# A convolution layer whose shared tap sum moves to ScalarE and GpSimd, one chunk ahead, with the running sum in PSUM

## The chip, the cores and the metric

The kernel runs on one core of a Trainium2 chip. A core has five engines with a queue each: TensorE (PE, matmuls), VectorE (DVE), ScalarE (ACT), GpSimd (POOL) and SyncE (SP), which issues the DMA transfers here. The engines work side by side and wait for one another by semaphores; within its queue each works in order. Two on-chip memories matter: SBUF, and PSUM with its eight banks of 128 x 512 float32, into which TensorE writes its products. The metric is the device time in microseconds from one launch; lower is better.

## The reference

A trunk of two layers over 1024 tokens of 1024 features. Layer 0 mixes tokens with a Conformer convolution, layer 1 with forgetting attention; each is followed by a cross-attention into 256 memory tokens and a squared-ReLU MLP. Only the convolution is touched:

```python
def conformer_conv(h, w_pw1, b_pw1, w_dw, b_dw, ln_g, ln_b, w_pw2, b_pw2):
    u = h @ w_pw1 + b_pw1
    a, gate = jnp.split(u, 2, axis=-1)
    u = a * jax.nn.sigmoid(gate)
    u = lax.conv_general_dilated(
        u, w_dw[:, None, :].astype(u.dtype),
        window_strides=(1,), padding=[(CONV_WIDTH - 1, 0)],
        dimension_numbers=("NWC", "WIO", "NWC"),
        feature_group_count=D_MODEL) + b_dw
    u = jax.nn.silu(layernorm(u, ln_g, ln_b))
    return u @ w_pw2 + b_pw2
```

## The kernel before

Features lie on the 128 partitions, so the 1024 features are eight chunks (`NCH`); tokens lie along the free axis, in two halves of 512. `X` holds the residual stream, one tile of 128 x 512 for each chunk and half. Float32 operands of the large products are split into a high and a low part (`split`, `low`, L147 to L152), and a product is three passes of matmuls, 128x128 by 128x512, summed in a PSUM bank (`product`, L266).

`conv_layer` (L293) normalizes `X` into `hs`, and then goes through the chunks:

- *The gate* (`gated_unit`, L362): for each half two products of 24 matmuls each, the gate first. ScalarE takes the sigmoid from the bank into `sg`, VectorE multiplies it with the other product (L370) into `u`, which keeps even and odd tokens in two planes with 15 zeros of padding in front of each (L301). There are two tiles `u`. The weights of the next chunk are loaded and split one chunk ahead (`gate_weights`).
- *The taps* (`convolve`, L386). Even and odd outputs share work: `d0` and `d1` are differences of neighbouring tokens (L393, L394), `both` is the sum over the odd plane with the pairwise tap sums (`tap_sums`), one product with the bias and 15 multiply-adds (L396, L400), and each of the two outputs then adds its own filters over the differences to it, 16 and 15 multiply-adds (L408). All of it is on VectorE; the running sums of the two outputs lie in two tiles of `X`, and the two runs of instructions alternate.
- Each finished chunk is added to `acc` (L354) for the layer norm's mean.

After the chunks `layer_norm` (L306) runs over both halves, and `linear` multiplies with `pw2` (L360).

Between the chunks the kernel prepares matrices for the two cross-attentions (`memory_matrices`, L433), which need nothing from the convolution: a generator, `prep`, with 32 steps, four for each of four heads and two layers: keys `kt`, values `vt`, then four results `o` from `wq` (L483) and four from `wo` (L501), each stored to DRAM by SP. Its products are in float32 with two matmul records each. Two steps are drawn in each pass over the chunks, four before them, the rest after the layer norm. They have four PSUM banks (`prep_pools(4)`), the gate has two (`banks(2)`), and two more serve small sums and broadcasts.

The order of each engine's instructions is fixed when the program is built. A list scheduler does it: what is traced earlier goes first among what is ready by the scheduler's own clock, and later work fills gaps. On the chip each queue keeps that order.

Of the kernel before, what the change touches and what calls it, by code (L numbers as in the profile page):

```python
# [12 lines left out]
F32 = mybir.dt.float32  # L13
F32R = mybir.dt.float32r
AF = mybir.ActivationFunctionType
ALU = mybir.AluOpType
# [3 lines left out]
P = 128  # L20
D = 1024
S = 1024
NCH = D // P
HALF = 512
# [6 lines left out]
TAPS = 31  # L31
PAD = TAPS - 1
# [4 lines left out]
HALVES = (slice(0, HALF), slice(HALF, S))  # L37
# [49 lines left out]
def trunk(ctx, tc, a, out):  # L87
    nc = tc.nc
    act, dve, pool, pe = nc.scalar, nc.vector, nc.gpsimd, nc.tensor
# [14 lines left out]
    def col(name, i):  # L104
        return par[:, COLS[name] + i : COLS[name] + i + 1]
# [22 lines left out]
    def open_x():  # L128
        xp = xpool.enter_context(tc.tile_pool(name="x", bufs=1, side="right", reuse_waits="tile"))
        return Halves(xp)  # L130

    def load_x(x, src, sl):
        for c in range(NCH):
            nc.sync.dma_start(x[:, c, sl], src[:, c, sl])

    X = open_x()
# [4 lines left out]
    def bank(p):  # L141
        return p.tile([P, HALF], F32, name="mm", tag="mm")

    def banks(n):
        return tc.tile_pool(name="pm", bufs=n, space=PSUM, reuse_waits="tile")
# [8 lines left out]
    def token_mean(acc):  # L154

        m = bank(ps)[:, : acc.shape[-1] // P]
        for b in range(m.shape[-1]):
            pe.matmul(m[:, b : b + 1], acc[:, b * P : (b + 1) * P], mean_col, start=True, stop=True)
        return m

    def spread(v):

        nb = v.shape[-1]
        r = bank(ps)
        with tc.high_priority(offset=SMALL_FIRST):
            for b in range(nb):
                pe.matmul(
                    r[:, b * P : (b + 1) * P], v[:, b : b + 1].to_broadcast([P, P]), ident,
                    start=True, stop=True,
                )  # L170
        return r[:, : nb * P]
# [56 lines left out]
    def operand_tile(p):  # L228
        return p.tile([P, 2, 2, HALF], F32R, name="op", tag="op")

    def operands():

        return [
            [t[:, i].rearrange("p h n -> p (h n)") for i in range(2)]
            for t in (operand_tile(opool) for _ in range(NCH))
        ]
# [53 lines left out]
        dve.tensor_tensor(X[:, m, sl], t, X[:, m, sl], op=ALU.add)  # L290


    def conv_layer(pm, prep):  # L293
        with tc.tile_pool(name="conv", bufs=2) as cp:
            for sl in HALVES:
                next(prep)
                load_x(X, a["xT"], sl)
            def padded():

                u = cp.tile([P, 2, (PAD + S) // 2], F32, name="u")  # L300
                pool.memset(u[:, :, : PAD // 2], 0.0)  # L301
                return u

            pairs = tap_sums(cp)

            def layer_norm(s, acc):  # L306

                nm = nrm.tile([P, 4], F32, name="nm")
                with tc.high_priority(offset=SMALL_FIRST):
                    dve.tensor_scalar(nm, token_mean(acc), -1.0, None, op0=ALU.mult)  # L310
                nmb = spread(nm)
                C = [X[:, m, HALVES[s]] for m in range(NCH)]
                for c in C:
                    dve.tensor_tensor(c, c, nmb, op=ALU.add)
                rb = spread(inverse_rms(C, LN_EPS))
                for m, c in enumerate(C):
                    dve.tensor_tensor(c, c, rb, op=ALU.mult)
                    act.activation(c, c, AF.Silu, bias=col("ln_b", m), scale=col("ln_g", m))
                    split(*(y.rearrange("p (n s) -> p s n", s=2)[:, s, :] for y in ss[m]), c)

            def add_x(m, sl, t):
                x = nrm.tile([P, HALF], F32, name="x", tag="t", bufs=4)
                nc.sync.dma_start(x, a["xT"][:, m, sl])
                dve.scalar_tensor_tensor(
                    X[:, m, sl], t, col("pw2_b", m), x, op0=ALU.add, op1=ALU.add
                )

            def gate_weights(m):
                return [weights(a["pw1"][2 * m + j]) for j in (1, 0)]

            hs = operands()
            ahead = gate_weights(0)
            u = padded()
            for sl in HALVES:
                normalize(hs, "mix0", sl)
                next(prep)
                gated_unit(pm, cp, 0, ahead, hs, u[:, :, PAD // 2 :], sl)
            acc = [cp.tile([P, HALF], F32, name=f"acc{s}", bufs=1) for s in range(2)]
            for m in range(NCH):
                if m:  # L340
                    u = padded()
                    for sl in HALVES:
                        gated_unit(pm, cp, m, ahead, hs, u[:, :, PAD // 2 :], sl)
                if m + 1 < NCH:
                    ahead = gate_weights(m + 1)
                for _ in range(2):
                    next(prep, None)

                convolve(cp, m, u, pairs[:, m])
                for s, sl in enumerate(HALVES):  # L350
                    if m == 0:
                        act.copy(acc[s], X[:, m, sl])
                    else:
                        dve.tensor_tensor(acc[s], acc[s], X[:, m, sl], op=ALU.add)  # L354
            ss = operands()
            for s in range(2):
                layer_norm(s, acc[s])
            for _ in prep:
                pass
            linear(pm, lambda m: weights(a["pw2"][m]), NCH, ss, add_x)  # L360

    def gated_unit(pm, cp, m, ws, hs, u, sl):  # L362
        sg = cp.tile([P, HALF], F32, name="sg")
        for j, w in zip((1, 0), ws):
            t = bank(pm)
            product(t, by_weights(w, hs, sl))
            if j:
                act.activation(sg, t, AF.Sigmoid, bias=col("pw1_b", NCH + m))
            else:
                dve.scalar_tensor_tensor(  # L370
                    u[:, :, sl.start // 2 : sl.stop // 2],
                    t.rearrange("p (n s) -> p s n", s=2), col("pw1_b", m),
                    sg.rearrange("p (n s) -> p s n", s=2), op0=ALU.add, op1=ALU.mult,
                )

    def tap_sums(cp):

        n = TAPS // 2
        w = par[:, COLS["dw_w"] : COLS["dw_w"] + NCH * TAPS].rearrange("p (m t) -> p m t", m=NCH)
        sums = cp.tile([P, NCH, n + 1], F32, name="sums", bufs=1)  # L380
        dve.tensor_copy(sums[:, :, n : n + 1], w[:, :, 2 * n :])
        two = w[:, :, : 2 * n].rearrange("p m (t s) -> p m t s", s=2)
        dve.tensor_tensor(sums[:, :, :n], two[:, :, :, 0], two[:, :, :, 1], op=ALU.add)
        return sums

    def convolve(cp, m, u, sums):  # L386


        n, k = S // 2, TAPS // 2
        even, odd = u[:, 0, :], u[:, 1, :]  # L390
        d0 = cp.tile([P, n + k], F32, name="d0")
        d1 = cp.tile([P, n + k - 1], F32, name="d1")
        dve.tensor_tensor(d0, even[:, : n + k], odd[:, : n + k], op=ALU.subtract)  # L393
        dve.tensor_tensor(d1, even[:, 1 : n + k], odd[:, : n + k - 1], op=ALU.subtract)  # L394
        both = cp.tile([P, n], F32, name="both")
        dve.tensor_scalar(  # L396
            both, odd[:, :n], sums[:, 0:1], col("dw_b", m), op0=ALU.mult, op1=ALU.add
        )
        for j in range(1, k + 1):
            dve.scalar_tensor_tensor(  # L400
                both, odd[:, j : j + n], sums[:, j : j + 1], both, op0=ALU.mult, op1=ALU.add
            )
        out = [X[:, m, sl] for sl in HALVES]
        for s, d, taps in ((0, d0, k + 1), (1, d1, k)):
            y = both
            for j in range(taps):
                w = col("dw_w", m * TAPS + 2 * j + s)
                dve.scalar_tensor_tensor(  # L408
                    out[s], d[:, j : j + n], w, y, op0=ALU.mult, op1=ALU.add
                )  # L410
                y = out[s]

# [13 lines left out]
    @contextmanager  # L428
    def prep_pools(n):
        with tc.tile_pool(name="prep", bufs=2) as pp, tc.tile_pool(name="pps", bufs=n, space=PSUM) as pq:  # L430
            yield pp, pq
# [928 lines left out]
            od[head // 2, i * HD : (i + 1) * HD, (b - 1) * P : (b + 1) * P], ol  # L1360
        )

    with prep_pools(4) as pools, banks(2) as pm:
        conv_layer(pm, chain(*(memory_matrices(*pools, l) for l in range(2))))
    sums = mem_attention(0)
    xd = dram.tile([P, NCH, S], F32, name="xd")
    first_normalized, first_weights = [], []
# [3 lines left out]
    for sl in HALVES:  # L1371
        rb = firsts if sl.start == 0 else spread(rms_of_sums(seconds, RMS_EPS))
        for c in range(NCH):
            y = X[:, c, sl]
# [71 lines left out]
```

## Time and profile before

| what | value |
|---|---|
| median of 3 runs | 2823.84 us (2814.29 to 2826.63) |
| profiled execution | 2825.31 us |
| its span, first to last instruction | 2823.3 us |
| mean granted TensorE clock | 0.991 |
| convolution layer: gates, taps and preparation | 60 to 395 us |
| layer norm | 389 to 443 us |
| product with `pw2` | to about 530 us |

A row of a group reads: line, engine, operation, output <- inputs, shape and count, then busy time, the mean of one in ns, and the idle time before it with what ended it. A row of the timeline reads: start, duration, engine, line, operation, count. The profile calls the weight load of a matmul PEld; it runs beside the matmuls.

### The profile page before, as it was taken

The page shows a single profiled execution, that of the slowest core. Times are in us where ns is not written, and L with a number is a line of the kernel's source. Part 1 is how long each engine was busy: PE and PEld are TensorE (multiplying, and loading weights), DVE is VectorE, ACT ScalarE, POOL GpSimd, SP SyncE. Part 2 cuts the span into 40 slices and gives each one's busy share as a digit, 9 for nine tenths or more (in the row PEclk, how much of TensorE's full clock was granted, in tenths as well). Part 3 has the DMA queues.
Part 4 walks back from the last instruction along what each step waited for, and adds up shares of the span by engine and source line. Part 5 has one row for each costly group of instructions (what it writes and reads, how often), then busy time and mean ns, then how long its engine had stood idle before and what let it go on. Part 6 is the DMA issues. An engine that isn't in the chain of part 4 may idle for free.

```text
span 2823.3 us, 36214 instructions
## 1 busy us (share of the span) xinstructions
PE 2740.8 (97%) x12968; PEld 2261.3 (80%) x12968; DVE 2030.9 (72%) x3358; ACT 1278.3 (45%) x2293; POOL 703.1 (25%) x473
## 2 busy tenths in 40 slices
PE   8999999999999999999899999989999999989998
PEld 6777777888888877888688888878888788878886
DVE  5999984555776576777788888875546855577776
ACT  5212143433555553333466666673423655543332
POOL 0000000000065625774000000000000365525773
PEclk9999999999999999999899999999999999999999
DMA  6334364322165585652222221243213455655651
GB/s 219 120 119 135 114 206 124 101 90 70 65 230 177 178 309 187 227 199 89 69 68 70 57 65 55 69 136 98 94 64 105 149 176 190 218 208 197 227 201 61
DMA packets 165428, 390.68 MB, mean 138 GB/s; under 512 B 17264, under 2 KB 46192, under 8 KB 164992
## 3 DMA queue, kind: packets, MB, share of 16 engines
q1 hardware_dynamic: 165248, 388.37, 40.9%
q8 instruction: 102, 1.67, 0.2%
q14 instruction: 78, 0.64, 0.1%
HBM read 270.79 MB, written 113.31 MB: 136 GB/s over the span
## 4 chain that ended last, share of the span: by engine, by line
PE 74%; DVE 12%; ACT 5%; DMA 5%; issue 3%; POOL 1%; SPq 0%; DVEq 0%; POOLq 0%; ACTq 0%
PE mm L1070 34%; PE mm L269 29%; PE mm L1255 5%; DVE w L148 2%; DVE op L148 2%; DVE x L408 1%; PE mm L1341 1%; DVE x L1310 1%; DMA ua<-x 1%; ACT x L1315 1%; PE mm L1353 1%; PE mm L1354 1%; DVE both L400 1%; DVE wl L148 1%; ACT pth L151 1%
## 5 line engine op out<-in xcount | busy, mean ns | idle before, releaser
L1070 PE MATMUL mm<-op,w 128*128 128x512 f32 x5424 | 1242.4, 391 | 24.5 <-ACT m L955 8.7
L1070 PEld LDWEIGHTS mm<-op,w 128*128 128x128 f32 x5424 | 1020.5, 189 | 243.2 <-ACT m L955 9.6
L269 PE MATMUL mm<-op,wh 128*128 128x512 f32 x1056 | 330.5, 394 | 4.2 <-DVE op L148 4.2
L148 DVE TENSOR_TENSOR w<-r,w 128x512 fp32r<-128x512 f32 x264 | 262.6, 998 | 30.5 <-ACT w L653 30.5
L653 ACT CAST w<-r 128x512 fp32r<-128x512 f32 x264 | 163.3, 622 | 262.0 <-PE mm L1070 233.2
L269 PEld LDWEIGHTS mm<-op,wh 128*128 128x128 f32 x1056 | 200.2, 190 | 48.5 <-DVE op L148 6.5
L1255 PE MATMUL mm<-op,wh 128*128 128x512 f32 x736 | 231.4, 396 | 0.0
L148 DVE TENSOR_TENSOR w<-t,w 128x512 fp32r<-128x512 f32 x180 | 178.2, 1005 | 63.2 <-ACT w L653 63.1
L269 PE MATMUL mm<-op,wl 128*128 128x512 f32 x528 | 210.5, 400 | 7.1 <-DVE wl L148 6.2
L207 POOL TENSOR_TENSOR r<-v,mhalf 128x4 f32<-128x4 f32 (+1 forms) x15 | 16.8, 1117 | 741.0 <-DVE v L205 741.0
L647 POOL TENSOR_TENSOR t<-r,t 128x512 f32<-128x512 f32 x104 | 174.9, 1681 | 91.4 <-DVE w L148 54.2
L653 ACT CAST w<-t 128x512 fp32r<-128x512 f32 x180 | 112.0, 622 | 169.8 <-PE mm L1070 140.6
L151 ACT CAST wh<-raw 128x1024 fp32r<-128x1024 f32 x96 | 100.7, 1050 | 193.8 <-PE mm L269 97.5
L865 POOL TENSOR_TENSOR x<-x,x 128x512 f32<-128x512 f32 x112 | 160.2, 1455 | 112.6 <-ACT x L878 101.6
L967 DVE TENSOR_TENSOR x<-mm,x 128x512 f32<-128x512 f32 x160 | 109.5, 684 | 91.1 <-PE mm L1070 73.7
L1255 PEld LDWEIGHTS mm<-op,wh 128*128 128x128 f32 x736 | 139.2, 189 | 26.7
L269 PE MATMUL mm<-op,xsh 128*128 128x512 f32 x512 | 158.0, 393 | 0.0
L1255 PE MATMUL mm<-op,wl 128*128 128x512 f32 x368 | 155.0, 421 | 1.9 <-ACT q L1275 1.9
L151 ACT CAST pth<-mm 128x512 fp32r<-128x512 f32 (+1 forms) x224 | 105.9, 495 | 108.5 <-PE mm L556 80.8
L408 DVE SCALAR_TENSOR_TENSOR x<-d,par,x 128x512 f32<-128x512 f32 x232 | 154.5, 746 | 0.0
L647 POOL TENSOR_TENSOR t<-r,r 128x512 f32<-128x512 f32 x52 | 80.2, 1542 | 295.1 <-DMA r<-in_ff_w 191.0
L1315 ACT ACTIVATE x<-x,nb 128x128 f32<-128x128 f32 (+7 forms) x128 | 99.5, 778 | 109.3 <-DVE nb L1313 100.0
(188 smaller groups left out, 4689.6 us busy)
## 6 DMA issues: line engine op xcount, KB each, us to landing
r<-in_ff_w SPq DMA_DIRECT2D x128, 512.0 KB, 4.0
op<-ua SPq DMA_DIRECT2D x80, 512.0 KB, 6.8
us<-x SPq DMA_DIRECT2D x128, 256.0 KB, 2.9
op<-us SPq DMA_DIRECT2D x64, 512.0 KB, 5.6
raw<-mvo SPq DMA_DIRECT2D x32, 512.0 KB, 3.4
ua<-ul SPq DMA_DIRECT2D x64, 256.0 KB, 2.2
ua<-uh SPq DMA_DIRECT2D x60, 256.0 KB, 2.3
raw<-in_pw SPq DMA_DIRECT2D x24, 512.0 KB, 4.7
```

Source lines behind the costliest of these rows:

```text
L148: dve.tensor_tensor(lo, src, hi.bitcast(F32), op=ALU.subtract)
L151: act.copy(hi, src)
L269: pe.matmul(out_ps, x, y, start=i == 0, stop=i == len(terms) - 1)
L400: dve.scalar_tensor_tensor(both, odd[:, j : j + n], sums[:, j : j + 1], both, op0=ALU.mult, op1=ALU.add)
L408: dve.scalar_tensor_tensor(out[s], d[:, j : j + n], w, y, op0=ALU.mult, op1=ALU.add)
L647: (dve if g in (2, 3, UP, UP + 1) else pool).tensor_tensor(t, raws[g, x], raws[g, y], op=ALU.subtract)
L653: act.copy(highs[n][0], raws[steps[n][:2]])
L865: eng.tensor_tensor(u[g, x], y1, y2, op=op_)
L967: dve.tensor_tensor(v, sums[key], v, op=ALU.add)
L1070: pe.matmul(sums[key], y, z, start=first and i == 0, stop=n == last_of[key] and i == len(terms) - 1, skip_group_check=True,)
L1255: pe.matmul(t, x, y, start=n == 0, stop=n == len(terms) - 1)
L1315: act.activation(x[:, :n], x[:, :n], AF.Exp, bias=nb, accum_out=rs)
```

## The change

The shared sum `both` leaves VectorE: `shared_sum` computes its 16 terms, ScalarE each product (`Identity` with scale and bias for the first, `Copy` with scale for the others, into six tiles `tap`), GpSimd the 15 additions. It is traced one chunk ahead of `convolve`. The gate is traced two chunks ahead, so there are three planes, padded once before the loop. In `convolve` the running sum of each output lies in one PSUM bank, `acc` of the pool `pc`, and only the last tap writes `X`; both outputs use the same bank in turn. `d0` and `d1` have one buffer each for two. The preparation's PSUM banks are three for four. The loop has one more pass, at m = -1, which gates chunk 1 and draws two preparation steps more.

```diff
-    def conv_layer(pm, prep):
+    def conv_layer(pm, pc, prep):
...
-            def padded():
-
-                u = cp.tile([P, 2, (PAD + S) // 2], F32, name="u")
+
+            planes = [cp.tile([P, 2, (PAD + S) // 2], F32, name=f"u{i}", bufs=1) for i in range(3)]
+            for u in planes:
                 pool.memset(u[:, :, : PAD // 2], 0.0)
-                return u
...
+            def gate(m, ws, sl):
+                gated_unit(pm, cp, m, ws, hs, planes[m % 3][:, :, PAD // 2 :], sl)
+
             hs = operands()
             ahead = gate_weights(0)
-            u = padded()
             for sl in HALVES:
                 normalize(hs, "mix0", sl)
                 next(prep)
-                gated_unit(pm, cp, 0, ahead, hs, u[:, :, PAD // 2 :], sl)
+                gate(0, ahead, sl)
             acc = [cp.tile([P, HALF], F32, name=f"acc{s}", bufs=1) for s in range(2)]
-            for m in range(NCH):
-                if m:
-                    u = padded()
-                    for sl in HALVES:
-                        gated_unit(pm, cp, m, ahead, hs, u[:, :, PAD // 2 :], sl)
-                if m + 1 < NCH:
-                    ahead = gate_weights(m + 1)
+            shared = shared_sum(cp, 0, planes[0], pairs[:, 0])
+            for m in range(-1, NCH):
+
+                if m + 2 < NCH:
+                    ahead = gate_weights(m + 2)
                 for _ in range(2):
                     next(prep, None)
-
-                convolve(cp, m, u, pairs[:, m])
+                if m + 2 < NCH:
+                    for sl in HALVES:
+                        gate(m + 2, ahead, sl)
+                if m < 0:
+                    continue
+                now = shared
+                if m + 1 < NCH:
+                    shared = shared_sum(cp, m + 1, planes[(m + 1) % 3], pairs[:, m + 1])
+
+                convolve(cp, pc, m, planes[m % 3], now)
...
-    def convolve(cp, m, u, sums):
+    def shared_sum(cp, m, u, sums):
+        n, k = S // 2, TAPS // 2
+        odd = u[:, 1, :]
+        both = cp.tile([P, n], F32, name="both")
+        act.activation(both, odd[:, :n], AF.Identity, scale=sums[:, 0:1], bias=col("dw_b", m))
+        for j in range(1, k + 1):
+            t = cp.tile([P, HALF], F32, name="tap", bufs=6)
+            act.activation(t, odd[:, j : j + n], AF.Copy, scale=sums[:, j : j + 1])
+            pool.tensor_tensor(both, both, t, op=ALU.add)
+        return both
+
+    def convolve(cp, pc, m, u, both):
         n, k = S // 2, TAPS // 2
         even, odd = u[:, 0, :], u[:, 1, :]
-        d0 = cp.tile([P, n + k], F32, name="d0")
-        d1 = cp.tile([P, n + k - 1], F32, name="d1")
+        d0 = cp.tile([P, n + k], F32, name="d0", bufs=1)
+        d1 = cp.tile([P, n + k - 1], F32, name="d1", bufs=1)
         dve.tensor_tensor(d0, even[:, : n + k], odd[:, : n + k], op=ALU.subtract)
         dve.tensor_tensor(d1, even[:, 1 : n + k], odd[:, : n + k - 1], op=ALU.subtract)
-        both = cp.tile([P, n], F32, name="both")
-        dve.tensor_scalar(
-            both, odd[:, :n], sums[:, 0:1], col("dw_b", m), op0=ALU.mult, op1=ALU.add
-        )
-        for j in range(1, k + 1):
-            dve.scalar_tensor_tensor(
-                both, odd[:, j : j + n], sums[:, j : j + 1], both, op0=ALU.mult, op1=ALU.add
-            )
-        out = [X[:, m, sl] for sl in HALVES]
+        acc = bank(pc)
         for s, d, taps in ((0, d0, k + 1), (1, d1, k)):
             y = both
             for j in range(taps):
+                o = X[:, m, HALVES[s]] if j == taps - 1 else acc
                 w = col("dw_w", m * TAPS + 2 * j + s)
-                dve.scalar_tensor_tensor(
-                    out[s], d[:, j : j + n], w, y, op0=ALU.mult, op1=ALU.add
-                )
-                y = out[s]
+                dve.scalar_tensor_tensor(o, d[:, j : j + n], w, y, op0=ALU.mult, op1=ALU.add)
+                y = acc
...
-    with prep_pools(4) as pools, banks(2) as pm:
-        conv_layer(pm, chain(*(memory_matrices(*pools, l) for l in range(2))))
+    with prep_pools(3) as pools, banks(2) as pm, banks(1) as pc:
+        conv_layer(pm, pc, chain(*(memory_matrices(*pools, l) for l in range(2))))
```

## The prediction

> **What bounds the kernel now.** First the page: the span, the busy shares, the chain that ended last.
>
> ```profile
> span 2823.3 us, 36214 instructions
> ...
> PE 2740.8 (97%) x12968; PEld 2261.3 (80%) x12968; DVE 2030.9 (72%) x3358; ACT 1278.3 (45%) x2293; POOL 703.1 (25%) x473
> ...
> PE 74%; DVE 12%; ACT 5%; DMA 5%; issue 3%; POOL 1%; SPq 0%; DVEq 0%; POOLq 0%; ACTq 0%
> ```
>
> TensorE is busy for 97% of the span, so all its idle time is 2823.3 - 2740.8 = 82.5 us. The change touches only the convolution layer; the view by windows cuts that layer out (window and its length, then for each engine busy us and instructions, granted clock, DMA share, GB/s).
>
> ```profile
> 0.00:60.00 60.00, 46.62 (x189) 36.96 (x190) 36.78 (x64) 32.81 (x62) 3.54 (x11) 0.94 0.63 222
> 60.00:100.00 40.00, 40.00 (x171) 31.90 (x170) 26.20 (x38) 7.15 (x10) 0.12 (x1) 1.00 0.43 132
> 100.00:200.00 100.00, 98.00 (x405) 75.63 (x404) 97.68 (x142) 21.32 (x35) 0.25 (x2) 1.00 0.34 109
> 200.00:300.00 100.00, 98.87 (x426) 79.81 (x425) 98.51 (x142) 22.23 (x36) 0.37 (x3) 1.00 0.39 127
> 300.00:395.00 95.00, 93.45 (x400) 73.68 (x400) 91.52 (x135) 21.79 (x39) 0.00 (x0) 1.00 0.57 178
> 395.00:440.00 45.00, 44.25 (x200) 33.17 (x199) 35.42 (x59) 33.27 (x58) 2.01 (x2) 1.00 0.56 178
> 440.00:530.00 90.00, 90.00 (x394) 73.12 (x394) 35.22 (x46) 26.74 (x38) 1.14 (x1) 1.00 0.34 100
> ```
>
> Two engines are full at once. From 100 to 395 us VectorE is busy for 287.7 of 295 us, and it alone runs the taps, so it looks like the bound. But TensorE is full too: from 60 to 530 us it idles 0 + 2.00 + 1.13 + 1.55 + 0.75 + 0 = 5.4 us. A busy PE need not be at its peak, so I check the pace. These are the PE groups, shapes apart, of 60 to 390 us:
>
> ```profile
> L269 PE MATMUL mm<-op,wh 128*128 128x512 f32 x480 | 147.9, 389 | 0.0
> L269 PE MATMUL mm<-op,wl 128*128 128x512 f32 x240 | 95.9, 400 | 1.7 <-DVE wl L148 1.7
> L269 PE MATMUL mm<-mem,praw 128*128 128x256 f32 x384 | 84.6, 379 | 0.5 <-DMA praw<-in_mem_wk 0.5
> L269 PE MATMUL mm<-praw,vt 128*128 128x512 f32 x92 | 41.9, 592 | 0.0
> L269 PE MATMUL mm<-kt,praw 128*128 128x256 f32 x169 | 40.0, 381 | 2.0 <-ACT o L483 2.0
> ```
>
> The three f32 groups take 84.6 + 41.9 + 40.0 = 166.5 us; about 162 us is left for the 720 gate matmuls, 0.225 us each. In 440 to 530 us, where VectorE is busy for only 35.2 us, 394 matmuls, nearly all of that same kind, fill 90 us: 0.228 us each. The pace is the same where VectorE is the full engine and where it is not, so **TensorE already does its work here as fast as it does anywhere**. What fills it is the memory-matrix preparation of both layers, which needs no convolution result and is slipped between the gate products. What is left of it fills TensorE during the layer norm, where it is busy for 44.25 of 45 us. From VectorE's timeline:
>
> ```profile
> 75.94 0.75 DVE L370 SCALAR_TENSOR_TENSOR u<-mm,par,sg 128x512 f32<-128x512 f32 x1 [2.56 <-PE mm L269]
> ...
> 329.10 19.30 DVE L408 SCALAR_TENSOR_TENSOR x<-d,par,x 128x512 f32<-128x512 f32 x29
> ...
> 349.52 0.74 DVE L370 SCALAR_TENSOR_TENSOR u<-mm,par,sg 128x512 f32<-128x512 f32 x1
> ...
> 354.74 11.77 DVE L400 SCALAR_TENSOR_TENSOR both<-u,sums,both 128x512 f32<-128x512 f32 x15
> ...
> 387.68 1.30 DVE L354 TENSOR_TENSOR acc<-acc,x 128x512 f32<-128x512 f32 x2
> ...
> 441.25 1.30 DVE L148 TENSOR_TENSOR op<-x,op 128x512 fp32r<-128x512 f32 x2 [1.20 <-ACT op L151]
> ```
>
> Chunk 0 is gated by 76.7 us, chunk 7 by 350.3; the convolution ends at 389.0, the norm at 442.6, a tail of 53.6 us. So both engines arrive at 442 us together: a balance of two bounds, of which the change lightens one.
>
> **The change part by part.** The prices (groups of VectorE and ScalarE in 0 to 440 us, and of GpSimd in the whole run; the ScalarE group L318 has two column operands, scale and bias):
>
> ```profile
> L408 DVE SCALAR_TENSOR_TENSOR x<-d,par,x 128x512 f32<-128x512 f32 x232 | 154.5, 746 | 0.0
> L400 DVE SCALAR_TENSOR_TENSOR both<-u,sums,both 128x512 f32<-128x512 f32 x120 | 90.2, 752 | 4.1
> L370 DVE SCALAR_TENSOR_TENSOR u<-mm,par,sg 128x512 f32<-128x512 f32 x16 | 11.6, 747 | 2.9 <-PE mm L269 2.9
> L501 ACT ACTIVATE o<-mm,mem_r 128x512 f32<-128x512 f32 x28 | 19.0, 685 | 47.9 <-DMA mqk<-o 23.1 <-DMA mvo<-o 18.4 <-PE mm L269 5.9
> L318 ACT ACTIVATE x<-x,par 128x512 f32<-128x512 f32 x16 | 12.1, 806 | 0.0
> L865 POOL TENSOR_TENSOR x<-x,x 128x512 f32<-128x512 f32 x112 | 160.2, 1455 | 112.6 <-ACT x L878 101.6 <-DMA us<-x 8.8
> L647 POOL TENSOR_TENSOR t<-r,t 128x512 f32<-128x512 f32 x104 | 174.9, 1681 | 91.4 <-DVE w L148 54.2 <-DMA ua<-ul 33.1
> ```
>
> *Shared sum off VectorE.* It loses 8 x 16 terms. Each add follows the one before on the same tile, and 15 took 11.77 us, 0.785 each; with the first term counted alike that is 100 us.
>
> *Running sum in PSUM.* The 31 filter taps of a chunk now form one chain on one bank: the first of the odd outputs must wait for the last of the even ones. Before, two chains on two X tiles alternated, 29 taps in 19.30 us, 0.666 each. A dependent tap goes at the 0.785 of L400, so 8 x 31 x 0.12 = 30 us come back. Net VectorE relief: about 70 us. A chain through PSUM is in no row. Single instructions that read PSUM cost the same (L370 747 ns, L408 746), so I take 0.785; the ends are 0.666 (nothing lost) and 1.0, the longest two-input 128x512 row (below).
>
> [...]
>
> *ScalarE and GpSimd.* Added on ScalarE: 8 products with scale and bias at about 0.81 us (L318) and 120 with scale at about 0.69 (L501): 89 us, on an engine busy for 65.3 of the 295 us. On GpSimd: 120 adds at 1.455 to 1.681, 175 to 202 us, on an engine that did almost nothing here; one chunk's sum is 15 adds, 22 to 25 us plus 1.5 for the first products, say 24.
>
> *GpSimd beside VectorE.* In 800 to 1200 us, where GpSimd adds, VectorE's groups read:
>
> ```profile
> L148 DVE TENSOR_TENSOR w<-r,w 128x512 fp32r<-128x512 f32 x81 | 81.2, 1004 | 13.5 <-ACT w L653 13.5
> L967 DVE TENSOR_TENSOR x<-mm,x 128x512 f32<-128x512 f32 x33 | 22.5, 683 | 19.6 <-PE mm L1070 12.2 <-POOL x L924 7.4
> ```
>
> Two SBUF inputs cost 1004 ns there, where 441.25 above shows 1.30 us for two; one input from PSUM costs 683. A tap with its sum in PSUM should therefore escape. Still exposed in a chunk are two differences, two first taps, the weights' two `low` and two `acc` adds, some 6.4 us; half more is 3.2 us a chunk, on VectorE only.
>
> [...]
>
> *TensorE.* Not one matmul is removed or added. The preparation over the whole run:
>
> ```profile
> L269 PE MATMUL mm<-mem,praw 128*128 128x256 f32 x512 | 116.7, 386 | 9.1 <-ACT mem L451 8.7 <-DMA praw<-in_mem_wk 0.5
> L269 PE MATMUL mm<-kt,praw 128*128 128x256 f32 x256 | 61.2, 385 | 6.0 <-ACT o L483 4.5 <-DMA praw<-in_mem_wq 1.4
> L269 PE MATMUL mm<-praw,vt 128*128 128x512 f32 x128 | 59.1, 594 | 0.0
> ```
>
> Its 32 steps are (116.7 + 61.2 + 59.1) / 32 = 7.4 us each. A gate has 96 matmuls, at 0.226 (between the two paces above) 21.7 us.
>
> *Order and path.* Per pass of the loop the order puts two preparation steps (14.8) and one gate (21.7) on TensorE: 36.5 us. VectorE needs 31 x 0.785 + 6.8 for the rest (two differences, two gated products, two `low`, two `acc`, most of a `kt`) + 3.2 = 34.3; GpSimd 24. TensorE leads. From 76.7 us seven gates follow: chunk 7 is gated at 76.7 + 7 x 36.5 = 332. Its shared sum ends at 356, its taps and adds 24.3 + 1.3 + 0.6 later, 382. Before, it was 389. The norm's tail of 53.6 us ends at 436 instead of 442.6, and until about 442 TensorE has the remaining preparation to do anyway. So 7 us of slack open up on VectorE's side and **nothing ends earlier**: the output projection (384 matmuls, 87 us) starts when TensorE has time.
>
> *Edits at nothing.* Three planes instead of two, five fewer pad memsets (125 ns each): off the path, and a gate two chunks ahead waits only for a plane whose differences are long formed. The preparation has three PSUM banks for four: a bank takes 8 x 0.237 = 1.9 us of matmuls, so two spare banks cover an eviction that is 3.8 us late; ScalarE already waits on the stores of `o` (23.1 + 18.4 us in the L501 row), so I charge 1 to 6 us and take 4. Recoverable on the other side: at most the 5.4 us of idle time and the 13.4 of the first 60, where the inputs are still on their way; I take 3. Sum: the profiled execution's 2825.3 (2.0 more than its span, 1.5 over the median of the three runs) - 3 + 4 = **2826 us**.
>
> **The rivals.**
>
> *A: ScalarE stands behind GpSimd.* ScalarE makes a product in 0.69 us, GpSimd takes 1.455 to 1.681; with six buffers it is held from about the tenth tap, up to a microsecond each time, and every eviction queued behind (`sg`, `o`, `vt`) is late. TensorE's queue is in order, so once an eviction is over 3.8 us late the next product stands. For it: ScalarE's load doubles, a bank is gone, `o` is waited for already. Against it: the waits come one at a time. At one or two such stops of 1.5 us a chunk it costs 12 to 24 us: 2837 to 2849. This is the slower side.
>
> *B: a PSUM tap is dear and VectorE bounds again.* VectorE starts its first taps at 76.7 + 24 = 101 and needs 31 t + 10 a chunk, the 10 being the 6.8 and 3.2 above. It decides where 101 + 8 x (31 t + 10) passes 389 + 7, that is t over 0.87 us. At t = 0.95 the convolution ends at 417, 21 us past it: 2847; at the upper end of 1.0 it ends at 429: 2859. Against it: L370.
>
> *C: the idle time goes.* If freer evictions let TensorE run through, at most the 5.4 us and about as much of the first 60 are won: 2815. It needs waits that VectorE causes, and the PE rows show 1.7 us of those; the others are DMA and ScalarE.
>
> *D: the change relieves an engine that does bound.* If TensorE's filler could be had later for nothing, the 70 us would count, up to 2755. The equal pace in two stages speaks against it, and no stall after 442 us is long enough to swallow preparation: the windows show 440 to 530 full.
>
> **How the numbers follow.** Forecast (2815 to 2837, balance kept) 0.55; A 0.20; B 0.12; C, at its price or, by another order later on, beyond it, 0.10; D 0.03. About 0.5%, 14 us, is what a measurement of this kernel can tell from no change; the three runs alone spread over 12 us. Two thirds of A and most of B pass it: slower 0.24. C beyond its price (0.07) and D: faster 0.10. Same: 0.66. The range takes in C's 2815 with a little of the runs' spread below it, A whole and B's lower half: 2811 to 2851.
>
> **What would show it.** Right: VectorE's busy share between 100 and 380 us falls to eight or nine tenths, TensorE's stays at nine and more, the last `acc` add comes before 389 and pw2's last matmul where it was. Taps in PSUM near 0.785 us from start to start. A shows as PE waits for ScalarE's `o`, `vt` or `sg` and as ScalarE waits for GpSimd's `both`; B as taps near 1 us with VectorE at ten tenths. A convolution layer shorter by over 14 us would prove the pace argument wrong.

## The result, and the profile after

The changed kernel takes 2906.15 us in the median of four runs (2902.68 to 2909.41), the kernel before 2822.45: a ratio of 1.030, with a 95% interval of 1.0273 to 1.0327. It is some 84 us slower, where 2826 us was forecast with 2851 as the upper end. Neither a rival nor the range held it.

The page of the changed kernel, the lines that answer to the first ones shown of before:

```profile
span 2903.1 us, 36411 instructions
...
PE 2764.2 (95%) x12968; PEld 2271.3 (78%) x12968; DVE 1961.1 (68%) x3230; ACT 1360.2 (47%) x2421; POOL 865.9 (30%) x588
...
PE 66%; DVE 15%; ACT 6%; POOL 5%; issue 4%; DMA 3%; SPq 0%; POOLq 0%; DVEq 0%; ACTq 0%
```

VectorE lost 70 us of work (2030.9 to 1961.1), the net relief that was reckoned before the 3.2 us a chunk for work beside GpSimd, and ScalarE and GpSimd gained 82 and 163. Yet the span grew by 79.8 us. It divides into two parts: TensorE idles 138.9 us for 82.5 before (56.4 more), and its unchanged 12968 matmuls are busy for 23.4 us longer. Its share of the chain fell from 74% to 66%, and GpSimd came into it. The windows of the layer (busy us and count of PE, PEld, DVE, ACT, POOL, then granted clock, DMA share, GB/s) show where:

```profile
100.00:200.00 100.00, 80.92 (x320) 62.35 (x318) 68.24 (x89) 36.60 (x57) 40.32 (x30) 0.91 0.27 84
200.00:300.00 100.00, 82.38 (x323) 63.99 (x324) 69.72 (x91) 37.02 (x61) 40.73 (x30) 0.90 0.29 95
300.00:395.00 95.00, 80.15 (x321) 62.33 (x320) 66.29 (x85) 35.36 (x55) 40.64 (x30) 0.93 0.30 94
395.00:440.00 45.00, 35.61 (x131) 26.25 (x130) 24.04 (x34) 17.24 (x30) 20.71 (x15) 0.90 0.49 152
440.00:530.00 90.00, 84.07 (x345) 61.56 (x344) 47.45 (x78) 47.11 (x82) 2.02 (x2) 0.98 0.56 171
```

From 100 to 440 us no engine is full any more. TensorE falls from 98 to 81 busy in a hundred, VectorE from 98 to 68, and GpSimd is at 40. Four engines with idle time and a longer stage point to a ring of waits, and the view of the waits names its links (who waited <- for whom: us in total, times, the longest):

```profile
POOL both L405 <- ACT tap L404: 202.2, 8, 29.4
DVE mm L421 <- POOL both L405: 117.6, 8, 17.5
...
PE mm L269 <- DVE u L377: 46.8, 7, 10.3
...
ACT both L401 <- DVE u L377: 9.4, 7, 2.2
```

GpSimd waits for ScalarE's products, ScalarE for VectorE's gated product `u`, TensorE for the same, and VectorE for GpSimd's sum. Each of these waits comes once in a chunk. VectorE's timeline shows how they close (start, duration, engine, line, operation, names, count):

```profile
120.11 0.75 DVE L377 SCALAR_TENSOR_TENSOR u<-mm,par,sg 128x512 f32<-128x512 f32 x1
...
143.78 0.76 DVE L421 SCALAR_TENSOR_TENSOR mm<-d,par,both 128x512 f32<-128x512 f32 x1 [17.47 <-POOL both L405]
144.57 9.46 DVE L421 SCALAR_TENSOR_TENSOR mm<-d,par,mm 128x512 f32<-128x512 f32 x12
153.94 0.75 DVE L377 SCALAR_TENSOR_TENSOR u<-mm,par,sg 128x512 f32<-128x512 f32 x1
154.60 1.54 DVE L421 SCALAR_TENSOR_TENSOR mm<-d,par,mm 128x512 f32<-128x512 f32 x2
...
163.85 0.75 DVE L377 SCALAR_TENSOR_TENSOR u<-mm,par,sg 128x512 f32<-128x512 f32 x1
...
187.71 0.76 DVE L421 SCALAR_TENSOR_TENSOR mm<-d,par,both 128x512 f32<-128x512 f32 x1 [12.12 <-POOL both L405]
```

At 120.9 chunk 1 is gated. Its shared sum takes until 143.8, and VectorE stands for it, 17.5 us of that with nothing to do. The gated products of chunk 2 (L377 at 153.94 and 163.85) stand behind that wait in VectorE's queue, between the taps of chunk 1. Only when they are through, at 164.6, can the sum of chunk 2 begin, which ends at 187.7. So a chunk takes the sum and most of the taps one after the other: 22.9 + 20.8 us, then 23.1 + 24.8 (to 212.5), 45.8 on average where 36.5 was reckoned for TensorE. GpSimd's and TensorE's rows of the same stretch, each from the timeline of its engine:

```profile
166.13 21.54 POOL L405 TENSOR_TENSOR both<-both,tap 128x512 f32<-128x512 f32 x15 [22.39 <-ACT tap L404]
```

```profile
154.75 0.79 PE L269 MATMUL mm<-op,wl 128*128 128x512 f32 x1 [3.32 <-DVE u L377]
```

GpSimd idles 22 us before its 15 adds because no plane is ready, and TensorE stands because, of the gate's two banks, the one that it needs next still holds the product that VectorE reads at 153.94.

### The profile page after: what moved, and what is told of

The parts are those of the page before. It is cut to its first block, busy times and chain, and to the rows that moved or that the text cites. A ratio compares the mean times of both kernels' runs of the same rounds, so it can differ in the third digit from the quotient of the medians.

```text
span 2903.1 us, 36411 instructions
## 1 busy us (share of the span) xinstructions
PE 2764.2 (95%) x12968; PEld 2271.3 (78%) x12968; DVE 1961.1 (68%) x3230; ACT 1360.2 (47%) x2421; POOL 865.9 (30%) x588
## 4 chain that ended last, share of the span: by engine, by line
PE 66%; DVE 15%; ACT 6%; POOL 5%; issue 4%; DMA 3%; SPq 0%; POOLq 0%; DVEq 0%; ACTq 0%
PE mm L1081 34%; PE mm L269 21%; PE mm L1266 5%; DVE mm L421 5%; POOL both L405 4%; DVE op L148 2%; DVE w L148 2%; PE mm L1352 1%; DVE x L1321 1%; PE mm L1364 1%; PE mm L1365 1%; ACT x L1326 1%; DVE wl L148 1%; PE mm L1316 1%; DMA x<-xs 1%
## 5 line engine op out<-in xcount | busy, mean ns | idle before, releaser
L269 PE MATMUL mm<-op,wh 128*128 128x512 f32 x1056 | 341.2, 405 | 4.1 <-DVE op L148 4.0
L269 PE MATMUL mm<-op,wl 128*128 128x512 f32 x528 | 217.3, 412 | 52.3 <-DVE u L377 46.8
L269 PEld LDWEIGHTS mm<-op,wh 128*128 128x128 f32 x1056 | 206.6, 196 | 52.1 <-DVE op L148 6.5
L1266 PE MATMUL mm<-op,wh 128*128 128x512 f32 x736 | 231.1, 395 | 0.0
L405 POOL TENSOR_TENSOR both<-both,tap 128x512 f32<-128x512 f32 x120 | 162.0, 1350 | 211.0 <-ACT tap L404 202.2
L421 DVE SCALAR_TENSOR_TENSOR mm<-d,par,mm 128x512 f32<-128x512 f32 x216 | 163.0, 755 | 5.8
L658 POOL TENSOR_TENSOR t<-r,r 128x512 f32<-128x512 f32 x52 | 81.4, 1565 | 286.4 <-DMA r<-in_ff_w 180.4
L269 PEld LDWEIGHTS mm<-op,wl 128*128 128x128 f32 x528 | 103.4, 196 | 80.2 <-DVE u L377 49.7
L1266 PEld LDWEIGHTS mm<-op,wh 128*128 128x128 f32 x736 | 139.3, 189 | 26.6
L1266 PE MATMUL mm<-op,wl 128*128 128x512 f32 x368 | 155.3, 422 | 1.9 <-ACT q L1286 1.9
```

What stands on the lines that cost most here:

```text
L269: pe.matmul(out_ps, x, y, start=i == 0, stop=i == len(terms) - 1)
L405: pool.tensor_tensor(both, both, t, op=ALU.add)
L421: dve.scalar_tensor_tensor(o, d[:, j : j + n], w, y, op0=ALU.mult, op1=ALU.add)
L658: (dve if g in (2, 3, UP, UP + 1) else pool).tensor_tensor(t, raws[g, x], raws[g, y], op=ALU.subtract)
L1266: pe.matmul(t, x, y, start=n == 0, stop=n == len(terms) - 1)
```

## The experiments

**The ring, opened by order alone.** VectorE's first tap of a chunk comes behind both gated products of the next chunk (an edge in the program order, with no semaphore and no new instruction; called the ordered kernel from here on):

```diff
+    gated = {}
...
                 dve.scalar_tensor_tensor(
                     u[:, :, sl.start // 2 : sl.stop // 2],
...
+                gated[m] = nc.cur_bb.bb.instructions[-1].name
...
                 dve.scalar_tensor_tensor(o, d[:, j : j + n], w, y, op0=ALU.mult, op1=ALU.add)
+                if j == s == 0 and m + 1 in gated:
+                    tc.add_manual_dep(
+                        nc.cur_bb.bb.instructions[-1], gated[m + 1],
+                        mybir.DependencyInfo(mybir.DependencyClass.NoSync, mybir.DependencyReason.DATA),
+                        reason="in order",
+                    )
```

> The kernel after, with one order added on VectorE: the first tap of a chunk comes behind both gated products of the next chunk. No instruction is added or removed. Theory Q (VectorE's queue: the gated product of the next chunk stands behind the wait for the shared sum, so gate, sum and taps form a ring of 23 + 24 us a chunk): the ring opens, a chunk takes TensorE's 36 to 37 us instead of 46, TensorE's granted clock returns to 1.0, 2820 to 2845 us. Rival S (the shared sum is simply too slow on ScalarE and GpSimd, wherever the products stand): 2890 us or more.

Measured: 2836.51 us, a ratio to before of 1.0059 (1.0036 to 1.0082). Some 70 of the 84 us are gone with the same number of instructions on TensorE, VectorE, ScalarE and GpSimd. The windows of 100 to 300 us and VectorE's timeline:

```profile
100.00:200.00 100.00, 99.03 (x411) 76.32 (x409) 83.13 (x102) 51.95 (x85) 56.48 (x42) 1.00 0.42 133
200.00:300.00 100.00, 99.91 (x432) 80.85 (x431) 86.50 (x110) 48.84 (x79) 52.91 (x41) 1.00 0.36 120
```

```profile
179.67 0.75 DVE L379 SCALAR_TENSOR_TENSOR u<-mm,par,sg 128x512 f32<-128x512 f32 x1 [2.52 <-PE mm L269]
180.33 0.75 DVE L424 SCALAR_TENSOR_TENSOR mm<-d,par,both 128x512 f32<-128x512 f32 x1
...
206.62 0.74 DVE L379 SCALAR_TENSOR_TENSOR u<-mm,par,sg 128x512 f32<-128x512 f32 x1
```

The second product of a chunk is through at 180.4, the first tap of the chunk before follows at once without a wait, and TensorE is busy for 199 of 200 us at a clock of 1.00. A chunk takes 36.1 us (second products at 107.77 and 324.24 us, six chunks apart) where it took 45.8. Theory Q holds; rival S, that the sum is too slow wherever the products stand, falls.

**The sum made shorter.** The kernel leaves 8 of the 15 additions out.

```diff
-            pool.tensor_tensor(both, both, t, op=ALU.add)
+            if j <= 7:
+                pool.tensor_tensor(both, both, t, op=ALU.add)
```

> The kernel after with 7 of the 15 additions of a shared sum; ScalarE still makes all products, 8 products are left out of the sum. Theory Q: the wait for the sum shrinks by 8 x 1.35 = 10.8 us a chunk, the ring from 46 to about 36 us, 2820 to 2850 us. Rival P (the loss comes from VectorE instructions slowed beside GpSimd, such as the second difference at 1.68 for 0.70 us, and from TensorE's lower clock in itself): half of a small effect goes, 2880 us or more.

Measured: 2856.16 us, 1.0125 (1.0097 to 1.0153), a little over the range of theory Q and far from rival P. The ring is still there, only shorter:

```profile
150.46 0.74 DVE L377 SCALAR_TENSOR_TENSOR u<-mm,par,sg 128x512 f32<-128x512 f32 x1
...
162.91 0.76 DVE L422 SCALAR_TENSOR_TENSOR mm<-d,par,both 128x512 f32<-128x512 f32 x1 [6.58 <-POOL both L406]
...
190.50 0.74 DVE L377 SCALAR_TENSOR_TENSOR u<-mm,par,sg 128x512 f32<-128x512 f32 x1
```

From the end of a chunk's second product to its first tap it is 11.7 us for 22.9. But the products of the next chunk now lie deeper among the taps, and the second of them ends 28.3 us behind the start of the first tap, so a chunk takes 40.0 us and not 36: that is what the expectation missed.

**The sum back on VectorE**, all else as after:

```diff
-        act.activation(both, odd[:, :n], AF.Identity, scale=sums[:, 0:1], bias=col("dw_b", m))
+        dve.tensor_scalar(
+            both, odd[:, :n], sums[:, 0:1], col("dw_b", m), op0=ALU.mult, op1=ALU.add
+        )
         for j in range(1, k + 1):
-            t = cp.tile([P, HALF], F32, name="tap", bufs=6)
-            act.activation(t, odd[:, j : j + n], AF.Copy, scale=sums[:, j : j + 1])
-            pool.tensor_tensor(both, both, t, op=ALU.add)
+            dve.scalar_tensor_tensor(
+                both, odd[:, j : j + n], sums[:, j : j + 1], both, op0=ALU.mult, op1=ALU.add
+            )
```

> The kernel after with the shared sum back on VectorE as before, everything else as after (gates traced two chunks ahead, PSUM running sum in one bank, three preparation banks, three planes). Theory Q: without the wait VectorE bounds, 31 x 0.79 + 16 x 0.785 + 6.8 = 44 us a chunk for 38 to 39 before, so the convolution ends some 40 us later than before: 2850 to 2875 us. Rival R (most of the loss comes from the PSUM chain, the lost bank or the new order of the gates): 2890 us or more.

Measured: 2836.97 us, 1.0061 (1.0042 to 1.0081), below both ranges. Without the wait for another engine the ring cannot form, and TensorE has no wait for `u` left between 60 and 530 us. The windows of 100 to 300 us:

```profile
100.00:200.00 100.00, 98.58 (x411) 76.69 (x410) 96.66 (x138) 23.52 (x38) 0.00 (x0) 1.00 0.40 130
200.00:300.00 100.00, 99.86 (x433) 81.15 (x432) 94.31 (x137) 20.78 (x34) 0.00 (x0) 1.00 0.37 123
```

The expectation had VectorE as the bound, but TensorE is the fuller of the two, and it gates a chunk in 36 us. The convolution ends at 407 us and not at 430: I had reckoned 44 us a chunk, and it took 41, since for long stretches taps and terms of the sum alternate, 0.66 us from start to start.

**Before, with the running sum in one PSUM bank and three preparation banks.**

```diff
-        out = [X[:, m, sl] for sl in HALVES]
+        acc = bank(pc)
...
-                dve.scalar_tensor_tensor(
-                    out[s], d[:, j : j + n], w, y, op0=ALU.mult, op1=ALU.add
-                )
-                y = out[s]
+                o = X[:, m, HALVES[s]] if j == taps - 1 else acc
+                dve.scalar_tensor_tensor(o, d[:, j : j + n], w, y, op0=ALU.mult, op1=ALU.add)
+                y = acc
...
-    with prep_pools(4) as pools, banks(2) as pm:
+    with prep_pools(3) as pools, banks(2) as pm, banks(1) as pc:
```

> The kernel before with one part of the change: the running sum in one PSUM bank, both outputs in turn, and three preparation banks for four. Taps one behind the other at 0.785 to 0.79 us for 0.666: 30 us more on VectorE. If VectorE and TensorE end together before, as the prediction said, TensorE runs out of filler and the kernel takes 2845 to 2865 us. Rival T (TensorE alone bounds and there is slack on VectorE): 2815 to 2832 us.

Measured: 2836.86 us, 1.0059 (1.0032 to 1.0086), between the two, with five runs spread from 2829 to 2851 us. This kernel, the one above and the ordered one all cost some 16 us, so I asked what they have in common. It is the running sum in PSUM, the lost bank, and in each one a PE wait of 7 to 11 us in the layer norm, in the ordered kernel this one:

```profile
412.51 6.67 PE L269 MATMUL mm<-praw,vt 128*128 128x512 f32 x8 [10.93 <-ACT o L503]
```

**Before with three banks for the preparation, and the ordered kernel with four.** In the second the running sum lies in one of the two banks of the small sums:

```diff
-    with prep_pools(4) as pools, banks(2) as pm:
+    with prep_pools(3) as pools, banks(2) as pm:
```

> The kernel before with three PSUM banks for the preparation instead of four, nothing else. Theory B (with the ring gone, what is left of the loss, 16 us, is the lost bank: in the layer norm ScalarE's queue holds an eviction for 14 us and three banks don't cover it): 2830 to 2842 us, with one long PE wait for ScalarE between 395 and 440 us. Rival F (the lost time is filler that other parts of the change use up earlier): 2814 to 2826 us.

```diff
-    with prep_pools(3) as pools, banks(2) as pm, banks(1) as pc:
-        conv_layer(pm, pc, chain(*(memory_matrices(*pools, l) for l in range(2))))
+    with prep_pools(4) as pools, banks(2) as pm:
+        conv_layer(pm, ps, chain(*(memory_matrices(*pools, l) for l in range(2))))
```

> The ordered kernel (first tap behind both gated products of the next chunk) with the running sum in one of the two banks of the small sums, which are free during the taps, so that the preparation has four banks again. Theory B: the 11 us wait in the layer norm goes, 2814 to 2828 us. Rival F: 2832 to 2842 us, as with three.

Measured: 2837.47 us, 1.0065 (1.0047 to 1.0084), and 2835.00 us, 1.0051 (1.0033 to 1.0069). The first speaks for theory B, the second against it. TensorE's timelines, before with three banks and then the ordered kernel with four:

```profile
413.89 5.65 PE L269 MATMUL mm<-mem,praw 128*128 128x256 f32 x16 [7.64 <-ACT o L501]
```

```profile
409.34 5.77 PE L269 MATMUL mm<-praw,vt 128*128 128x512 f32 x8 [8.40 <-ACT o L503]
```

The wait is there with four banks too, so the lost bank alone doesn't make it, as theory B had it. It does bear on it: before has no PE wait for ScalarE over 2.0 us between 60 and 530 us, and the first kernel differs from it in the bank alone. What both rows name is ScalarE's eviction of `o`.

**Two small banks, so that the taps alternate**, on top of the order and four banks; and before with only the PSUM sum and four banks:

```diff
-        acc = bank(pc)
+        accs = [bank(pc) for _ in range(2)]
...
-            y = both
+            y, acc = both, accs[s]
```

> The kernel with order and four preparation banks, and the running sums of the two outputs in both banks of the small sums, so that their taps alternate. Taps fall from 0.79 to 0.67 us, 30 us less on VectorE. If TensorE bounds the layer, as the prediction said, that brings nothing: within 5 us of the one with one bank, 2812 to 2828 us. If VectorE still bounds it: 15 us and more below that one.

> The kernel before with the running sum of both outputs in one bank of the small sums, four preparation banks kept. The convolution ends some 20 us later, as it did with three banks (410 for 389 us). If the filler ends with the norm before, TensorE idles for most of that after 442 us: 2830 to 2842 us. If the bank was the whole loss of the run with three banks: 2815 to 2826 us.

Measured: 2829.83 us, 1.0033 (1.0018 to 1.0048), and 2828.19 us, 1.0032 (1.0018 to 1.0047). The second lies between its two ranges and settles little: with no bank lost to the preparation some 9 us are lost all the same, while its longest PE wait for ScalarE is 3.7 us. Its convolution ended at 402 us and not at 410, its norm 3 us behind that of before. The first came out 2 us above its range and 5.2 below the kernel with one bank, far from the 15 of the rival. Its windows of 100 to 300 us:

```profile
100.00:200.00 100.00, 100.00 (x418) 78.11 (x417) 78.20 (x111) 53.85 (x87) 57.42 (x44) 1.00 0.40 133
200.00:300.00 100.00, 100.00 (x435) 81.53 (x434) 77.33 (x107) 49.46 (x79) 53.81 (x41) 1.00 0.38 125
```

VectorE has more than a fifth of its time free, and TensorE, full in every microsecond, issues 418 and 435 matmuls where before it issued 405 and 426. TensorE has no idle time left to win there.

**ScalarE's evictions first.** In the layer norm of the ordered kernel ScalarE has 12 us of activations and casts in a row, and an eviction of the preparation stands behind them:

```profile
399.94 1.52 ACT L317 ACTIVATE x<-x,par 128x512 f32<-128x512 f32 x2
...
410.45 1.65 ACT L182 ACTIVATE t<-x 128x512 f32<-128x512 f32 x3
412.01 0.45 ACT L503 ACTIVATE o<-mm,par 128x256 f32<-128x256 f32 x1
```

The evictions get priority over them, first in the ordered kernel with three banks:

```diff
-                    act.copy(o, t)
+                    with tc.high_priority(offset=SMALL_FIRST):
+                        act.copy(o, t)
...
-                        act.activation(o[:, f, :], t[:, f, :], AF.Copy, scale=gain)
+                        with tc.high_priority(offset=SMALL_FIRST):
+                            act.activation(o[:, f, :], t[:, f, :], AF.Copy, scale=gain)
...
-                    act.activation(
-                        o, t.rearrange("p (b n) -> p b n", b=4), AF.Copy,
-                        scale=mem_r[0][:, mc : mc + 1],
-                    )
+                    with tc.high_priority(offset=SMALL_FIRST):
+                        act.activation(
+                            o, t.rearrange("p (b n) -> p b n", b=4), AF.Copy,
+                            scale=mem_r[0][:, mc : mc + 1],
+                        )
```

> The ordered kernel with three preparation banks, and the preparation's evictions on ScalarE (o, vt) ahead of the layer norm's activations where both are ready. Theory L (what is left of the loss is one PE wait of 11 us in the layer norm, where ScalarE's queue runs 14 us of activations ahead of an eviction): the wait falls under 2 us and the kernel takes 2816 to 2828 us. Rival (the wait comes from the number of banks or from the end of the filler): 2832 us or more, with another wait in its place.

> The ordered kernel with two small banks for the running sums and four preparation banks, with the evictions first. Theory L: its wait of 7.5 us goes, 2812 to 2824 us, the same as before or up to 5 us below it, since TensorE has nothing else to give up in this layer. If VectorE's relief counted after all: under 2808 us.

> The kernel before with the preparation's evictions first. It has no long wait in its layer norm, only 5.4 us of TensorE idle time from 60 to 530 us: 2813 to 2824 us, the same as before. If the order of ScalarE matters elsewhere too: 6 us and more away from it.

Measured: 2826.41 us, 1.0021 (1.0005 to 1.0037); with two small banks and four preparation banks 2820.60 us, 0.9991 (0.9974 to 1.0008); before with the same priority 2823.46 us, 1.0004 (0.9987 to 1.0021). The window of the layer norm, in the ordered kernel without and then with the priority:

```profile
395.00:440.00 45.00, 32.65 (x142) 24.77 (x143) 30.36 (x50) 31.75 (x52) 1.58 (x2) 0.85 0.44 141
```

```profile
395.00:440.00 45.00, 42.43 (x183) 31.33 (x182) 30.24 (x50) 33.16 (x57) 2.02 (x2) 0.96 0.59 185
```

TensorE is busy for 42.4 us where it was 32.7, and the long wait is gone. Theory L holds for some 10 of the 16 us. The best of all these kernels is level with before; none is faster.

**Other steps in the layer norm**, on the kernel with two small banks:

```diff
-                for _ in range(2):
+                for _ in range(2 if m >= 0 else 0):
                     next(prep, None)
```

> The kernel with two small banks and four preparation banks, evictions as they were, and the first pass of the loop (m = -1) draws no preparation step, so that other steps fall into the layer norm. If the wait there depends on which steps meet it: it changes in length, 2814 to 2828 us without it. If it is there whatever steps come: 7 to 11 us of wait again, 2826 to 2836 us.

Measured: 2830.87 us, 1.0030 (1.0014 to 1.0047). The long wait fell from 7.5 to 2.5 us (now for `vt`), so it does depend on which steps meet the norm, but from 60 to 100 us TensorE was busy for only 35.3 of 40 us, at a granted clock of 0.91, and the time stayed, in the range of the other reading. How much of the last 16 us the lost bank makes by itself stays open: before with three banks shows the loss, but in it the steps that meet the norm moved too.

## Why the prediction was wrong

**The pace argument was right.** TensorE bounds this layer at its usual pace: with 20 us in a hundred taken off VectorE, the kernel with two small banks and the evictions first takes 0.9991 of before. That relief on VectorE brings nothing was the forecast's core. One reading on the way is a little off: in 60 to 390 us TensorE is busy for 325.3 us, so some 159 us are left for the 720 gate matmuls and not 162, 0.221 us each. They are no slower than the 0.228 of the later stage, and the argument stands.

**The prices were right.** A tap in a dependent chain through PSUM goes at 0.789 us (14 in 11.05) for the assumed 0.785. A product on ScalarE took 716 ns for 690, the first one 813 for 806, an add on GpSimd 1.35 us for 1.455 to 1.681, a shared sum 23 us for 24. For work beside GpSimd 3.2 us a chunk were charged; the groups that it named came out 1.6 us a chunk longer in the changed kernel and 2.2 in the ordered one. The groups of ScalarE and GpSimd:

```profile
L404 ACT ACTIVATE tap<-u,sums 128x512 f32<-128x512 f32 x120 | 81.5, 716 | 25.3 <-POOL both L405 25.1
L405 POOL TENSOR_TENSOR both<-both,tap 128x512 f32<-128x512 f32 x120 | 162.0, 1350 | 211.0 <-ACT tap L404 202.2
```

So rival B is out.

**The step that failed is "Order and path".** It let TensorE lead with 36.5 us a chunk; the reason stands under "Edits at nothing": "a gate two chunks ahead waits only for a plane whose differences are long formed". That is true of the plane, and it leaves out the queue. The change adds a wait to VectorE, its first tap for the shared sum, and the prediction never asked what stands behind the waiting instruction: the gated products that free TensorE's banks and feed the next shared sum. Traced two chunks ahead, they ran one chunk ahead, among the taps. In place of TensorE's 36.5 us the ring set the pace, with 45.8 us a chunk. The ordered kernel shows that this costs some 70 us, and there the path is near the one forecast: chunk 7 is gated at 325 us (332 forecast), the convolution ends at 390 (382), and VectorE is busy for 83 to 87 us in a hundred beside a full TensorE.

**The term for three banks looks too small, though no run takes it by itself in the changed kernel.** It was charged with 4 us, in a range of 1 to 6. Before with three banks is some 18 us slower than before (1.0065), and the ordered kernel some 16. Some 10 us of these 16 are evictions held back in ScalarE's queue in the layer norm, behind the norm's own activations and not behind late stores of `o`; how much of the rest the bank makes stays open.

**Rival A named the wrong queue.** ScalarE did stand behind GpSimd, 41 times, 25.1 us in all and never longer than 1.0 us. TensorE's waits for ScalarE's `o` and `vt` between 60 and 530 us grew to 13.4 us from 2.0, which lies in A's 12 to 24 us, but no run shows that GpSimd made them: in the ordered kernel, where ScalarE stood behind GpSimd 32 times, they come to 4.8 us before the layer norm. The 46.8 us for VectorE's `u` weigh more. The same question put to VectorE would have found the ring.

**The rest**, some 6 us between the ordered kernel with evictions first and before (1.0005 to 1.0037), isn't taken apart. It is gone with two small banks for the sums and four preparation banks (0.9974 to 1.0008).

## What to carry to other kernels

When a step moves to a helper engine, the engine that takes the result may get a wait, and all that stands behind it in that queue gets it too, as on VectorE here (117.6 us for GpSimd's sum): look there for the instruction that feeds the helper's next round. Two engines that are full at once need a look at the pace of both, since relief for one of them may bring nothing, as here (0.9991 of before with 20 us in a hundred off VectorE). Being traced ahead is not running ahead; the timeline of the queue shows the distance that is left.

## What the runs showed of the hardware

**In the changed kernel an idle TensorE cost twice.** After a wait of 3.3 us TensorE came back at a granted clock of 0.50, not 1.00. Windows of 4 us in the changed kernel:

```profile
148.00:152.00 4.00, 3.43 (x16) 2.50 (x14) 3.82 (x6) 0.54 (x1) 0.00 (x0) 1.00 0.00 0
152.00:156.00 4.00, 1.25 (x3) 1.07 (x4) 3.89 (x6) 1.08 (x2) 0.00 (x0) 0.79 0.00 0
156.00:160.00 4.00, 4.00 (x15) 3.19 (x15) 3.86 (x7) 0.00 (x0) 0.00 (x0) 0.78 0.00 0
160.00:164.00 4.00, 4.00 (x20) 3.43 (x19) 3.93 (x6) 1.05 (x1) 0.00 (x0) 1.00 0.28 97
```

TensorE's rows of the same stretch:

```profile
156.19 0.63 PE L269 MATMUL mm<-op,wl 128*128 128x512 f32 x1
156.62 1.05 PE L269 MATMUL mm<-op,wh 128*128 128x512 f32 x2
157.47 0.54 PE L269 MATMUL mm<-op,wl 128*128 128x512 f32 x1
...
158.31 0.39 PE L269 MATMUL mm<-op,wl 128*128 128x512 f32 x1
158.54 0.61 PE L269 MATMUL mm<-op,wh 128*128 128x512 f32 x2
159.00 0.39 PE L269 MATMUL mm<-op,wl 128*128 128x512 f32 x1
```

In windows of 1 us the granted clock is 0.50 from 155 to 157 us and 1.00 again from 158 us. Three gate matmuls take 1.28 us before (156.19 to 157.47) and 0.69 us after (158.31 to 159.00). There are seven such gaps, of 3.3 to 10.3 us, one a chunk, each with a clock of 0.50 in some windows of 1 us behind it, and with them the same matmuls were busy for 23.4 us longer. In the ordered kernel, where the clock of 100 to 300 us is 1.00, they are busy for 2742.0 us, 1.2 us longer than before. In the gap shown TensorE starts again at 154.75, some 3 us before the clock is back.

**VectorE beside GpSimd.** Some instructions with two inputs in SBUF took longer beside GpSimd's adds, up to more than double; not all did: while the 15 adds from 166.13 to 187.67 us ran, an `acc` add at 173.20 took 0.69 us and the second difference right behind it 1.78 us. On average, in the changed kernel the second difference took 1681 ns (702 before), in the ordered kernel the first taps 1123 (750 before) and the `acc` adds 1154 (686 before), while a tap with its sum in PSUM stayed at 754:

```profile
L414 DVE TENSOR_TENSOR d<-u 128x526 f32<-128x526 f32 x8 | 13.4, 1681 | 0.0
```

```profile
L424 DVE SCALAR_TENSOR_TENSOR mm<-d,par,mm 128x512 f32<-128x512 f32 x216 | 162.9, 754 | 6.2
L424 DVE SCALAR_TENSOR_TENSOR mm<-d,par,both 128x512 f32<-128x512 f32 x16 | 18.0, 1123 | 0.3
...
L361 DVE TENSOR_TENSOR acc<-acc,x 128x512 f32<-128x512 f32 x14 | 16.2, 1154 | 0.2
```

The second difference is longer by 0.98 us on average, less than a whole GpSimd add (1.35 us).
